# A tenth seven-product pair ahead of the attention, and low weight parts added up by a DMA

## Chip, cores and metric

The kernel runs on one core of one Trainium2 chip. The metric is the device time of one execution in microseconds. The kernel before took 1343.89 us, the median of 3 runs (1341.61 to 1345.63).

## What is computed

One layer of a decoder trunk on 1024 tokens with 1024 channels, in float32. An input projection gives queries, keys and values for two token mixers and two blocks of 1024 gate columns. One mixer is differential attention (4 heads, full causal softmax), the other a sliding-window attention (8 heads, window 128). Each mixer's output goes through its own matrix and is weighted by the sigmoid of its gates; the two are summed, mixed and added to the input. A gated MLP with a short convolution and a last norm follow.

```python
xn = rmsnorm(x, norm_mix_w[l])
proj = xn @ w_in[l]
da_q, da_k, da_v, sw_q, sw_k, sw_v, g_da, g_sw = split_cols(proj)
y_da = diff_attention(da_q, da_k, da_v, lam, lam_init, subln_w[l])
y_sw = sliding_window_attention(sw_q, sw_k, sw_v, sinks[l])
merged = jax.nn.sigmoid(g_da) * (y_da @ w_br_da[l]) + jax.nn.sigmoid(g_sw) * (y_sw @ w_br_sw[l])
x = x + merged @ w_mix_out[l]
```

## The kernel before

Data is kept transposed: channels on the 128 partitions, tokens along the row. Every float32 operand of a large product is split into a high part (a copy rounded to float32r, by ScalarE) and a low part (the operand minus its high part, by VectorE), and a product is three matmuls of 128x512: high by high, high by low, low by high (`mm3`, L202 to L211; the same in `product`, L906 to L923).

The 34 column blocks of the input projection, 128 columns each, are numbered 0 to 33; 18 to 33 are the 16 gate blocks, in the code simply "gates". `plan` (L280) sorts them into three kinds:

- `plain`: five blocks, computed directly at the start.
- `pairs`: two blocks at a time by a Strassen-like scheme of seven products (P1 to P7) of half size in place of eight. A pair takes 7 products x 4 chunks of channels x 3 matmuls = 84 matmuls; two blocks alone take 2 blocks x 2 halves of the tokens x 8 chunks x 3 = 96. The sums of weights that the scheme needs are made by GpSimd (`sum_pair`, L93, four additions a pair at L103 and L107 to L109), the high and low parts by ScalarE and VectorE (`split_pair`, L112, lines 127 and 128), and VectorE puts the seven products together (`recombine`, L454, seven additions, and one copy by ScalarE). A pair of gates is then stored to memory (`gd`) from SP's queue, L448.
- the remaining gates (23 to 33, eleven of them): computed directly, but later, between the steps of the attention. `back_half` (L559) computes one half of one gate: 24 matmuls, a copy out of PSUM by ScalarE (L565) and a store to `gd` from ScalarE's queue (L566).

`HALVES` says how many such halves are written behind each step of the attention: the first entry before it starts, then six rows of eight steps (four heads of differential attention, `u` = 0 to 3, and two groups of sliding-window heads, `u` = 4 and 5), and the last entry behind the attention, while its output is loaded. A scheduler then fixes each engine's order ahead of time, in the priority in which the code is written but taking later work that is ready where an engine would stand idle; so the halves do not stay where they are written.

A weight block is loaded by `load_w` (L167): raw weights by a DMA on SP's queue into one of three `raw` buffers, the high part by ScalarE (`wh`, L174), the low part by VectorE (`wl`, L176). Both have two buffers, and `ahead` (L70) starts the next block's loading when the present one is begun. The kernel before issues no DMA from GpSimd.

A step of differential attention (`da_step`, L622) is two score products, a masked minimum on VectorE (L640), the exponential on ScalarE (L641), a combination on VectorE (L646), transposes on TensorE (L652) and again high and low parts (L654, L655); every second step ends in the product with the values (`da_av`, L657). A sliding-window step (`sw_step`, L713) does the same for four heads; one head's scaling is done by GpSimd (L738, three others on the same line by VectorE). GpSimd also clears a part of each `aT` tile (L619). The stacks of queries and keys (`u` tiles, L576 and L586) come from memory (`qd`) and take the place of operands of the projection.

After the attention, `rest` (L766) loads the gates back (`gr`, L793), scales them on GpSimd (L794), and merges the two branches.

Of the kernel before, what the change touches and what calls it, by code (L numbers as in the profile page):

```python
# [10 lines left out]
F32 = mybir.dt.float32  # L11
F32R = mybir.dt.float32r
AF = mybir.ActivationFunctionType
ALU = mybir.AluOpType
# [6 lines left out]
KC = D // P  # L21
# [12 lines left out]
HOLD = 1  # L34
LAM_INIT = 0.2

HALVES = ((2,), (0, 0, 0, 0, 1, 1, 0, 0), (0, 0, 0, 0, 1, 0, 0, 1), (0, 0, 0, 0, 1, 0, 1, 0), (0, 0, 0, 1, 1, 0, 1, 0), (1, 0, 0, 1, 0, 1, 1, 0), (1, 0, 1, 1, 0, 0, 1, 0), (3,))
NEGMASK = 1e30


# [4 lines left out]
class Trunk:  # L45
# [121 lines left out]
    def load_w(self, src, nk=KC, eng=None, pool=None, raw=None):  # L167

        nc = self.nc
        if raw is None:  # L170
            raw = self.load_raw(src, nk)
        pool, h, l = pool or (self.wp, "wh", "wl")
        wh = self.tl(pool, [P, nk, P], h, F32R)
        self.hi = nc.scalar.copy(wh, raw)  # L174
        wl = self.tl(pool, [P, nk, P], l, F32R)
        self.lo = (eng or nc.vector).tensor_tensor(wl, raw, wh.bitcast(F32), ALU.subtract)  # L176
        return wh, wl

# [101 lines left out]
    def plan(self):  # L280

        self.kind = {m: "q" if m < 4 or 12 <= m < 16 else "k" if m < 8 or m == 16 else "v" if m < 18 else "g" for m in range(34)}


        self.plain = [0, 4, 8, 18, 20]
        self.pairs = [(1, 5), (9, 2), (6, 10), (3, 7), (11, 12), (13, 16), (17, 14), (15, 19), (21, 22)]
        gates = list(range(23, 34))
        self.back = []
        todo = [(m, hf) for m in gates for hf in range(2)]
        for steps in HALVES:  # L290
            self.back.append([[todo.pop(0) for _ in range(n)] for n in steps])
        assert not todo
        src = [(self.w_in[m], KC) for m in self.plain]
        src += [((self.w_in[a], self.w_in[b]), "pair") for a, b in self.pairs]
        src += [(self.w_in[m], KC) for m in gates]
        src += [(self.w_br[m], KC) for m in range(KC)]
        self.mix_order = [m for k in range(4) for m in (k, k + 4)]
        src += [(self.w_mix[m], KC) for m in self.mix_order]
        src += [((self.w_up[j], self.w_up[j + NF]), "pair") for j in range(NF)]


        n = N1 // 2
        self.pieces = [(m, c) for m0 in (4, 0) for c in range(2) for m in range(m0, m0 + 4)]
        src += [(self.w_dn[m:m + 2, :, n * c:n * c + n, :].rearrange("m p k c -> p m k c"), 2 * n) for m, c in self.pieces[::2]]
        pairs = [(self.w_dn[m, :, N1:N1 + 8, :], self.w_dn[m + 4, :, N1:N1 + 8, :]) for m in range(4)]
        src.insert(len(src) - 2, (pairs[0], "sums"))
        src += [(self.w_dn[m, :, N1:N1 + 8, :], 8) for m in range(4)]
        src += [(pairs[0], "rest")] + [(p, "pair", True, 1) for p in pairs[1:]]
        src += [((self.w_dn[m, :, N2:, :], self.w_dn[m + 4, :, N2:, :]), "second", m) for m in range(4)]
        src += [(self.sd[m], 8) if m < 2 else (self.sd[m], "idle") for m in range(4)]  # L310
        self.wsrc, self.wq, self.deep = src, [], False
# [1135 lines left out]
```

## Time and profile before

| | us |
|---|---|
| median of 3 runs | 1343.89 |
| lowest, highest of them | 1341.61, 1345.63 |
| the profiled execution, its own time | 1342.84 |
| its span, first to last instruction | 1340.6 |
| outside the span | 2.2 |

The page of the profile gives the busy time of each engine (PE is TensorE, PEld its weight loads, DVE VectorE, ACT ScalarE, POOL GpSimd, SP the engine that issues most DMAs), the span in 40 slices, the chain of work that ended last, and the costliest groups of instructions. Matmul records overlap, since a matmul starts before the one ahead of it has drained: the pace of TensorE is read from the starts, not from the durations. The table of windows gives each engine's busy time in a chosen stretch of the span. Projection with its pairs runs to 239 us, the attention to about 506, the merging of the branches to about 600.

### The profile page before, as it was taken

How to read it: one execution, taken by the hardware profiler on the slowest of the kernel's cores; microseconds unless marked ns; L12 is line 12 of the kernel's file. 1: busy time of each engine (PE TensorE's matmuls, PEld its weight loads, DVE VectorE, ACT ScalarE, POOL GpSimd, SP SyncE). 2: the span in 40 equal slices, each digit the busy share in tenths (PEclk: the TensorE clock that was granted, in tenths of full speed). 3: DMA queues.
4: the chain of work that ended last, by engine and by line, in shares of the span. 5: the costliest groups of instructions: out<-in, count | busy, mean ns of one | idle time of the engine just before them, and what ended most of it. 6: DMA issues, size and time to landing. Idle time of an engine off the chain costs nothing.

```text
span 1340.6 us, 17301 instructions
## 1 busy us (share of the span) xinstructions
PE 1319.9 (98%) x6264; PEld 1097.0 (82%) x6264; DVE 1069.3 (80%) x1605; ACT 621.2 (46%) x1019; POOL 497.0 (37%) x365
## 2 busy tenths in 40 slices
PE   8999999999999999999999999999999999999997
PEld 6888888888888777878888888888888888888787
DVE  8847775289889876465678999999999997978985
ACT  9432232276667765333444443444443444323454
POOL 0336553001102124651446555655565510215422
PEclk9999999999999999999999999999999999999998
DMA  7423443876553235334432222222222229671333
GB/s 258 145 107 143 156 158 141 246 182 186 144 135 124 97 119 203 141 110 157 126 110 95 78 95 79 94 68 90 90 85 80 85 82 337 214 263 63 112 124 126
DMA packets 63045, 182.64 MB, mean 136 GB/s; under 512 B 6896, under 2 KB 15216, under 8 KB 62960
## 3 DMA queue, kind: packets, MB, share of 16 engines
q1 hardware_dynamic: 51504, 164.13, 37.5%
q10 hardware_dynamic: 11456, 17.41, 3.6%
q8 instruction: 49, 0.80, 0.3%
q14 instruction: 36, 0.29, 0.1%
HBM read 130.66 MB, written 50.86 MB: 135 GB/s over the span
## 4 chain that ended last, share of the span: by engine, by line
PE 87%; POOL 4%; DVE 4%; DMA 3%; ACT 1%; issue 1%; POOLq 0%; SPq 0%; ACTq 0%; DVEq 0%
PE t L920 13%; PE t L921 13%; PE t L922 13%; PE g L209 3%; PE t L914 3%; PE g L210 3%; PE g L211 3%; PE sc L636 3%; PE y L1159 2%; PE d L1159 2%; DMA gr<-gd 2%; PE sc L211 2%; PE sc L209 2%; PE sc L210 2%; PE d L920 2%; PE d L921 2%
## 5 line engine op out<-in xcount | busy, mean ns | idle before, releaser
L1089 ACT ACTIVATE c<-us,vecs 128x512 f32<-128x512 f32 x80 | 61.3, 780 | 133.2 <-POOL us L1083 129.2
L1091 DVE SCALAR_TENSOR_TENSOR c<-us,vecs,c 128x512 f32<-128x512 f32 x160 | 110.4, 747 | 8.6 <-ACT c L1089 8.5
L1083 POOL TENSOR_TENSOR us<-us,rstd 128x1024 f32<-128x1024 f32 x38 | 99.7, 2643 | 4.5 <-DVE us L469 2.4
L128 DVE TENSOR_TENSOR sl<-sf,sh 128x1024 fp32r<-128x1024 f32 x62 | 87.6, 1415 | 11.5 <-ACT sh L127 11.5
L127 ACT CAST sh<-sf 128x1024 fp32r<-128x1024 f32 x62 | 63.3, 1048 | 60.2 <-PE t L921 43.7
L176 DVE TENSOR_TENSOR wl<-raw,wh 128x1024 fp32r<-128x1024 f32 (+2 forms) x46 | 55.7, 1210 | 31.8 <-ACT wh L174 20.2
L128 DVE TENSOR_TENSOR wl<-raw,wh 128x1024 fp32r<-128x1024 f32 (+1 forms) x35 | 76.3, 2180 | 3.7 <-ACT wh L127 3.6
L103 POOL TENSOR_TENSOR sf<-rv 128x512 f32<-128x512 f32 x30 | 41.3, 1378 | 100.9 <-DVE sl L128 57.8
L174 ACT CAST wh<-raw 128x1024 fp32r<-128x1024 f32 (+2 forms) x46 | 46.1, 1001 | 61.8 <-PE sc L210 30.5
L209 PE MATMUL g<-xh,wh 128*128 128x512 f32 x176 | 70.6, 401 | 0.1
L211 PE MATMUL g<-xh,wl 128*128 128x512 f32 x176 | 70.3, 400 | 0.0
L210 PE MATMUL g<-xl,wh 128*128 128x512 f32 x176 | 70.3, 399 | 0.0
L108 POOL TENSOR_TENSOR sf<-raw,rv 128x512 f32<-128x512 f32 x30 | 40.7, 1358 | 65.3 <-DVE sl L128 65.3
L619 POOL MEMSET aT<- 128x128 f32 x32 | 6.2, 206 | 151.6 <-PE t L665 101.3
L640 DVE CUSTOM_DVE_ANT_0 L<-sc,bias 128x128 f32<-128x128 f32 (+7 forms) x64 | 47.7, 751 | 17.0 <-PE sc L636 13.7
L641 ACT ACTIVATE L<-L,sm 128x128 f32<-128x128 f32 (+7 forms) x64 | 49.6, 778 | 20.0 <-DVE sm L640 17.3
L794 POOL TENSOR_TENSOR gr<-gr,rstd 128x1024 f32<-128x1024 f32 x16 | 40.6, 2540 | 42.5 <-DMA gr<-gd 42.3
L1093 ACT ACTIVATE c<-c 128x512 f32<-128x512 f32 x40 | 24.0, 599 | 60.7 <-DVE c L1091 60.7
L128 DVE TENSOR_TENSOR wl<-rv,wh 128x512 fp32r<-128x512 f32 x30 | 49.3, 1642 | 3.5 <-ACT wh L127 3.5
L636 PE MATMUL sc<-u,u 128*128 128x512 f32 (+2 forms) x192 | 49.8, 358 | 0.0
L211 PE MATMUL sc<-mh,wl 128*128 128x512 f32 x126 | 49.1, 390 | 0.5 <-DVE wl L176 0.5
L209 PE MATMUL sc<-mh,wh 128*128 128x512 f32 x126 | 49.0, 389 | 0.0
(527 smaller groups left out, 4400.3 us busy)
## 6 DMA issues: line engine op xcount, KB each, us to landing
u<-qd SPq DMA_DIRECT2D x72, 256.0 KB, 6.6
raw<-in_w_in SPq DMA_DIRECT2D x25, 512.0 KB, 4.2
raw<-in_w_up SPq DMA_DIRECT2D x23, 512.0 KB, 3.5
hr<-hd SPq DMA_DIRECT2D x46, 256.0 KB, 4.9
hd<-c SPq DMA_DIRECT2D x22, 512.0 KB, 2.6
rv<-in_w_up SPq DMA_DIRECT2D x21, 512.0 KB, 3.5
raw<-in_w_down SPq DMA_DIRECT2D x19, 512.0 KB, 4.2
gr<-gd SPq DMA_DIRECT2D x16, 512.0 KB, 3.7
```

Of the source, the lines that this page charges most:

```text
L127: i = nc.scalar.copy(hi, src)
L128: j = nc.vector.tensor_tensor(lo, src, hi.bitcast(F32), ALU.subtract)
L209: nc.tensor.matmul(ps, wh[:, kc + o, :], ah, start=first and n == 0, stop=False)
L210: nc.tensor.matmul(ps, wh[:, kc + o, :], al, start=False, stop=False)
L211: nc.tensor.matmul(ps, wl[:, kc + o, :], ah, start=False, stop=last and n == len(kcs) - 1)
L636: nc.tensor.matmul(sc[:, lo + n0:lo + n1], qs, k[c][part][:, n0:n1], start=part == 0, stop=part == 1)
L920: nc.tensor.matmul(ps, ah[:, k, :], bh, start=first and n == 0, stop=False, skip_group_check=skip)
L921: nc.tensor.matmul(ps, ah[:, k, :], bl, start=False, stop=False, skip_group_check=skip)
L922: i = nc.tensor.matmul(ps, al[:, k, :], bh, start=False, stop=last and n == len(ks) - 1, skip_group_check=skip)
L1083: (nc.vector if j == 0 else nc.gpsimd).tensor_tensor(u[:, 2:], u[:, 2:], self.rstd, ALU.mult)
L1089: nc.scalar.activation(c, u[:, o + 2:o + 2 + H2], AF.Identity, bias=self.vecs[:, C_CB + m:C_CB + m + 1], scale=col(m, 2))
L1091: nc.vector.scalar_tensor_tensor(c, u[:, o + k:o + k + H2], col(m, k), c, ALU.mult, ALU.add)
```

## The change

Gates 23 and 24 become a tenth pair, computed ahead of the attention. Nine gates (25 to 33) stay behind it, so 18 halves in place of 22: `HALVES` loses one in each of the rows of `u` = 0, 3, 4 and 5. For the last seven of these gates (27 to 33) the low part is made in another way: ScalarE writes the negated high part into the low part's tile, and a DMA issued by GpSimd adds the raw weights to it there. Gates 25 and 26 keep VectorE's subtraction, and so does every other weight.

```diff
-HALVES = ((2,), (0, 0, 0, 0, 1, 1, 0, 0), (0, 0, 0, 0, 1, 0, 0, 1), (0, 0, 0, 0, 1, 0, 1, 0), (0, 0, 0, 1, 1, 0, 1, 0), (1, 0, 0, 1, 0, 1, 1, 0), (1, 0, 1, 1, 0, 0, 1, 0), (3,))
+HALVES = ((2,), (0, 0, 0, 0, 0, 1, 0, 0), (0, 0, 0, 0, 1, 0, 0, 1), (0, 0, 0, 0, 1, 0, 1, 0), (0, 0, 0, 0, 1, 0, 1, 0), (1, 0, 0, 1, 0, 0, 1, 0), (1, 0, 0, 1, 0, 0, 1, 0), (3,))
...
         wl = self.tl(pool, [P, nk, P], l, F32R)
+        if eng == "adding":
+            nc.scalar.mul(wl, wh.bitcast(F32), -1.0)
+            nc.gpsimd.dma_start(wl, raw, accum_op=ALU.add)
+            return wh, wl
         self.lo = (eng or nc.vector).tensor_tensor(wl, raw, wh.bitcast(F32), ALU.subtract)
...
-        self.pairs = [(1, 5), (9, 2), (6, 10), (3, 7), (11, 12), (13, 16), (17, 14), (15, 19), (21, 22)]
-        gates = list(range(23, 34))
+        self.pairs = [(1, 5), (9, 2), (6, 10), (3, 7), (11, 12), (13, 16), (17, 14), (15, 19), (21, 22), (23, 24)]
+        gates = list(range(25, 34))
...
-        src += [(self.w_in[m], KC) for m in gates]
+        src += [(self.w_in[m], KC) for m in gates[:2]] + [(self.w_in[m], KC, "adding") for m in gates[2:]]
```

## The prediction

> **What bounds the kernel.** I read the page first: the busy times and the chain that ended last.
>
> ```profile
> span 1340.6 us, 17301 instructions
> PE 1319.9 (98%) x6264; PEld 1097.0 (82%) x6264; DVE 1069.3 (80%) x1605; ACT 621.2 (46%) x1019; POOL 497.0 (37%) x365
> PE 87%; POOL 4%; DVE 4%; DMA 3%; ACT 1%; issue 1%; POOLq 0%; SPq 0%; ACTq 0%; DVEq 0%
> ```
>
> TensorE sets the time nearly everywhere. An average hides what a stage leaves to the other engines, so next the table of windows, cut at the last three pairs, the wait for the attention's stacks (239 to 269), the four heads `u` = 0 to 3, the two sliding-window groups and the merging. Columns: stretch, its length, busy time of PE, PEld, DVE, ACT, POOL with counts, granted clock, DMA share, GB/s.
>
> ```profile
> 201.00:220.00 19.00, 19.00 (x86) 15.73 (x85) 12.30 (x13) 5.21 (x6) 9.87 (x5) 1.00 0.38 138
> 220.00:239.00 19.00, 19.00 (x85) 15.74 (x84) 10.49 (x17) 3.52 (x5) 1.28 (x6) 1.00 0.39 139
> 239.00:269.00 30.00, 30.00 (x142) 24.89 (x141) 6.32 (x16) 7.34 (x17) 0.20 (x2) 1.00 0.97 265
> 269.00:299.00 30.00, 30.00 (x189) 26.11 (x188) 28.27 (x76) 22.20 (x53) 1.24 (x7) 1.00 0.75 188
> 299.00:335.00 36.00, 36.00 (x236) 32.03 (x234) 31.16 (x82) 24.61 (x58) 3.75 (x12) 1.00 0.66 179
> 335.00:368.00 33.00, 32.95 (x211) 28.50 (x211) 28.91 (x73) 22.57 (x52) 3.02 (x8) 1.00 0.56 148
> 368.00:404.00 36.00, 35.97 (x242) 32.08 (x240) 31.04 (x91) 22.74 (x58) 3.45 (x8) 1.00 0.55 140
> 404.00:452.00 48.00, 46.92 (x271) 38.16 (x271) 40.89 (x151) 35.03 (x104) 9.21 (x10) 1.00 0.37 121
> 452.00:506.00 54.00, 53.38 (x271) 42.03 (x270) 43.07 (x136) 37.48 (x98) 12.38 (x9) 1.00 0.30 98
> ```
>
> Two things are to be seen. In the attention TensorE is full (idle 0.05 + 0.03 + 1.08 + 0.62 = 1.78 us from 269 to 506), but VectorE is close behind it: 28.27 + 31.16 + 28.91 + 31.04 + 40.89 + 43.07 = 203.3 us of those 237, or 86%. The gates are what keeps TensorE full there. And from 239 to 269 VectorE has little to do and the DMA engines are at 0.97: the stacks are loading, and gates fill TensorE.
>
> TensorE's pace is read from starts in its timeline, since records overlap:
>
> ```profile
> 219.97 0.39 PE L920 MATMUL t<-xh,wh 128*128 128x512 f32 x1
> 239.01 0.39 PE L209 MATMUL g<-xh,wh 128*128 128x512 f32 x1
> 249.89 0.38 PE L606 MATMUL t<-ident,f 128*128 128x128 f32 x2
> ```
>
> The last pair runs from 219.97 to 239.01, 19.04 us for its 84 matmuls, 0.2267 us each. The 48 matmuls of the first gate take 239.01 to 249.89, 10.88 us, the same pace. So both forms of work run undisturbed at it.
>
> **The pair.** Four halves leave the attention: 4 x 24 x 0.2267 = 21.8 us of TensorE work. A pair is added ahead of it: 19.04 us. Net 12 matmuls, **-2.72 us**, if both stretches stay full. For the pair that holds. What it needs from the other engines:
>
> ```profile
> L108 POOL TENSOR_TENSOR sf<-raw,rv 128x512 f32<-128x512 f32 x30 | 40.7, 1358 | 65.3 <-DVE sl L128 65.3
> L128 DVE TENSOR_TENSOR sl<-sf,sh 128x1024 fp32r<-128x1024 f32 x62 | 87.6, 1415 | 11.5 <-ACT sh L127 11.5
> L467 DVE TENSOR_TENSOR us<-t,u 128x512 f32<-128x512 f32 x31 | 21.4, 691 | 0.9
> ```
>
> Four additions on GpSimd (5.4 us), three and a half low parts (about 5 us) and seven additions (4.8 us) on VectorE. The parts of the tenth pair are made while the ninth is computed (220 to 239: VectorE 10.49 of 19, GpSimd 1.28), and both are pairs of gates without the extra splitting that keys and queries need. The pair before that left VectorE 12.30 of 19 with TensorE full, so I cost this at nothing; without cover the dearest piece is one subtraction of 1.4 us. Its stores to `gd` go from SP ahead of the stacks, as the ninth pair's do now.
>
> **The low parts.** What is replaced, and the load that is nearest to the new DMA:
>
> ```profile
> L176 DVE TENSOR_TENSOR wl<-raw,wh 128x1024 fp32r<-128x1024 f32 x10 | 12.1, 1215 | 13.2 <-PE t L606 11.0 <-ACT wh L174 2.2
> L174 ACT CAST wh<-raw 128x1024 fp32r<-128x1024 f32 x37 | 38.8, 1049 | 50.1 <-PE sc L210 30.5 <-PE g L210 8.1 <-PE d L921 4.7
> DMA to landing us min/median/max: 2.6/4.0/9.0
> 250.94 1.23 DVE L176 TENSOR_TENSOR wl<-raw,wh 128x1024 fp32r<-128x1024 f32 x1 [11.04 <-PE t L606]
> 261.97 0.39 PE L209 MATMUL g<-xh,wh 128*128 128x512 f32 x1
> ```
>
> The first row is of 239 to 506 alone, the third of the 512 KB weight loads of L164, the last two of the timelines. Seven subtractions, 7 x 1.215 = 8.5 us, leave VectorE between 269 and 506 (of the ten rows two lie before 269, one is of the weights behind the gates). ScalarE gets seven more passes, 7 x 1.049 = 7.3 us: its sum there is 164.6 us of 237, and 171.9 of 215 is 80%, still below VectorE. No row shows a DMA that GpSimd issues and that adds. By the loads it lands 2.6 to 9.0 us after issue; I take 9.0 for the first, which falls into the stretch with the DMA engines at 0.97. The third gate's low part was ready at 252.2, and its first matmul ran at 261.97 (the 97th of the gates): 9.8 us of slack against 1.05 + 9.0 - 1.2 = 8.9 us. Hidden, barely; later gates have a half's spacing more. Issuing costs GpSimd something unknown: nothing at the low end, at the high end a whole pass over such a tile, the 2.54 us of L794 below, seven times, on an engine that is busy 33 of 237 us.
>
> The wait that comes with it: the DMA waits on GpSimd's queue for ScalarE's second pass. Behind it stand the clearing of `aT` and one head's scaling.
>
> ```profile
> POOL aT L619 <- PE t L665: 101.3, 14, 34.7
> L738 POOL TENSOR_SCALAR L<-L,sw 128x256 f32<-128x256 f32 x14 | 14.3, 1024 | 58.2 <-DVE sw L735 30.2 <-DVE sw L729 8.9 <-PE t L755 8.7
> L794 POOL TENSOR_TENSOR gr<-gr,rstd 128x1024 f32<-128x1024 f32 x16 | 40.6, 2540 | 42.5 <-DMA gr<-gd 42.3
> SPq L164 <- DVE wl L176: 69.9, 6, 20.4
> 494.99 3.58 SPq L793 DMA_DIRECT2D gr<-gd x2
> ```
>
> GpSimd waits for others there far more than they for it, so I price that at 0, with 4 late gates x 2.5 us = 10 us, if each pass held up a sliding-window step, as its far end. The raw buffer is held until the DMA has read it, and SP's queue waits for those buffers (fourth row); behind the longest waits stand only weights and then the loads of L793, and the last wait before them is for a weight that VectorE still subtracts. Price 0.
>
> By the Trainium skill, DMA: Bandwidth & Descriptors, section Anatomy of one DMA — SWDGE (gpsimd) path, such a DMA takes about 2.0 us plus its bytes over 436 GB/s, an estimate of 3.2 us here; by it the sum would be the same. The skill speaks against the change in SBUF — State Buffer, section Who interferes with whom: a VectorE instruction in a two-port mode locks GpSimd out, and a DMA from GpSimd then waits for its descriptors. That rule is the rival "late low parts" below; no row of this trace shows such a wait, since GpSimd issues none.
>
> **The attention with fewer gates.** This is the disputed term. From 269 on VectorE keeps 203.3 - 8.5 = 194.8 us of work, and TensorE wants to be through in 237 - 21.8 = 215.2. That asks VectorE for a share of 90.5%, now 85.8%. What share it can reach bounds the price from both sides. At 94.2%, the row 269 to 299 with TensorE full, it needs 206.8 us: price 0. At 88.4%, the mean of the four heads (119.4 of 135), 220.4: price 5.2. In those heads TensorE, not VectorE, was the limit, so 88.4% is a floor rather than a ceiling; but they include the slack places between heads that will not go away. I take the middle, **+2.5 us**.
>
> **Sum.** 1342.84 - 2.72 + 2.5 = **1342.6 us** against the profiled execution's own time, itself 1.05 below the median of the runs, 1343.89. A measurement of this kernel can tell about 0.3%, 4 us, from no change; the forecast is no change that can be told.
>
> **Rivals.**
> 1. *The softmax takes over: slower.* VectorE's share stays at 85.8%, because its idle time is a step's own chain (minimum, exponential, transposes, two parts) and not TensorE's queue. Then 194.8 / 0.858 = 227.0 us, price 11.9: 1342.84 - 2.72 + 11.9 = **1352.0**. For it: in the two sliding-window stretches VectorE is at 84 of 102 us, and TensorE already idles 1.70. Against it: TensorE runs its queue in order, with gates ahead of the attention's own matmuls, so part of that idle time is the gates' doing. It is slower by over 0.3% from a share of 87.8% down (221.9 us, price 6.7).
> 2. *The relief wins: faster.* VectorE's lighter load ends the 1.78 us of idle TensorE too, and nothing opens: 1342.84 - 2.72 - 1.78 = **1338.3**. For it: the sliding-window stretches hold four of the seven subtractions. Against it: it asks for 90.5% without a gap.
> 3. *Late low parts: slower.* GpSimd is held up, by VectorE or by its own queue, and the DMA lands after twice the longest load, 18.0 us. The third gate's low part is then 1.05 + 18.0 - 1.2 - 9.8 = 8.1 us late, while there are only gates to run: 1342.6 + 8.1 = **1350.7**. Against it: 9.8 us of slack, and the scheduler can put score products first.
> 4. *The pair doesn't gain what it says.* Its parts come late and the 2.72 us are lost in its first products: **1345.3**. Against it: TensorE full in the stretch at 12.30 of 19 us of VectorE and 9.87 of GpSimd.
>
> **Chances.** Forecast 0.43 (1340 to 1346), rival 1 0.26, rival 2 0.18, rival 3 0.06, rival 4 0.07. Faster by over 0.3% (below 1339.9) needs rival 2 nearly whole: 0.17. Slower by over 0.3% (above 1347.9): most of rivals 1 and 3, 0.28. Within: 0.55. The range goes from rival 2 to rival 1: 1338.3 to 1352.0.
>
> **What would show it.** After: a tenth stretch of 19.0 us ahead of the first gate, which starts at 258; VectorE at about 90% from then + 30 us to the end of the attention; the attention's end at 506 - 2.7 + 2.5. If VectorE's share there stays near 86% and TensorE idles over 7 us, rival 1; if TensorE waits at L211 for `wl`, rival 3; if TensorE idles under 1 us, rival 2. If the projection's end comes later than 258.2, rival 4. The step I trust least is the share of 90%.

## The result, and the profile after

| | us |
|---|---|
| after, median of 6 runs | 1354.82 (1351.43 to 1356.68) |
| before, median of 6 runs beside them | 1343.77 (1340.64 to 1345.63) |
| ratio, 95% interval | 1.0084, 1.0071 to 1.0097 |
| profiled execution after, its span | 1351.43, 1349.6 |

The change costs 0.84%, 11.05 us of the medians. The time lies above the range of the prediction, and on the side to which it gave 0.28. The profiled execution is the fastest of its six, so the traces explain 9.0 us of span (1349.6 against 1340.6), and the rest is spread between executions.

The page of the kernel after: span, busy times, and the chain that ended last.

```profile
span 1349.6 us, 17324 instructions
PE 1320.8 (98%) x6252; PEld 1096.1 (81%) x6252; DVE 1067.5 (79%) x1607; ACT 627.3 (46%) x1025; POOL 508.7 (38%) x376
PE 85%; DVE 4%; POOL 4%; DMA 3%; ACT 2%; issue 1%; POOLq 0%; SPq 0%; ACTq 0%; DVEq 0%
```

Twelve matmuls fewer, as the change says, and yet TensorE is no less busy and the span is longer: the averages of the page do not show where the time goes. TensorE's timeline after the change gives the marks: start of the last pair, first gate, first product of the merging.

```profile
238.36 0.39 PE L924 MATMUL t<-xh,wh 128*128 128x512 f32 x1
...
257.40 0.39 PE L213 MATMUL g<-xh,wh 128*128 128x512 f32 x1
...
516.02 0.39 PE L200 MATMUL sc<-yh,wh 128*128 128x512 f32 x1
```

And the last of them before the change:

```profile
506.40 0.39 PE L196 MATMUL sc<-yh,wh 128*128 128x512 f32 x1
```

The tenth pair takes 257.40 - 238.36 = 19.04 us, to the hundredth what was forecast. From the first gate to the merging the kernel took 506.40 - 239.01 = 267.39 us, and now 516.02 - 257.40 = 258.62. That is 8.77 less, where 21.8 us of gates were taken out. The first gate starts 18.39 us later, and 18.39 - 8.77 = 9.6 us are lost by the merging; behind it 0.6 come back. All of the loss lies between the attention's start and its end.

The table of windows shows it. "The stretch" is from now on the time from 30 us after the first gate to the merging. Before:

```profile
269.00:506.40 237.40, 235.62 (x1409) 199.25 (x1409) 203.74 (x607) 164.73 (x420) 33.05 (x53) 1.00 0.50 140
```

After, whole, and in parts (the last one cut at 520):

```profile
287.40:516.00 228.60, 218.93 (x1319) 184.08 (x1319) 196.83 (x606) 166.69 (x423) 36.66 (x58) 0.99 0.57 153
...
387.00:423.00 36.00, 33.03 (x228) 28.52 (x228) 30.54 (x88) 23.30 (x59) 3.17 (x7) 1.00 0.50 121
423.00:470.00 47.00, 43.06 (x244) 34.26 (x243) 44.19 (x177) 37.10 (x111) 11.01 (x12) 1.00 0.42 126
470.00:520.00 50.00, 47.29 (x235) 37.30 (x234) 36.91 (x110) 36.50 (x87) 11.42 (x9) 0.97 0.43 132
```

VectorE's share was 203.74 / 237.40 = 85.8% and is 196.83 / 228.60 = 86.1%: it did not move. TensorE's idle time went from 1.8 to 9.7 us, nearly all of it in the last three parts (2.97 + 3.94 + 2.71), that is from the fourth head on. The first three heads still fill TensorE with nearly as many gate matmuls as before (129 against 136, counted in the stretches of the three heads); the fourth head holds 17 in place of 42, and the two sliding-window groups 169 in place of 231. The four halves that were taken away are missing at the end. What TensorE waits for most in the stretch, after the change:

```profile
PE t L759 <- DVE aT L753: 3.1, 5, 1.0
PE g L213 <- ACT g L569: 1.8, 2, 0.9
PE t L668 <- DVE aT L659: 1.2, 2, 0.9
```

The first and the third row are waits for the low parts of the transposed softmax weights, VectorE's work; with a smaller row of the same kind they make 4.7 us of the 9.4 that all rows of this view add up to. No row of it is a wait at L215 for `wl`. The low parts by DMA, in the groups and in the rows of `wl`:

```profile
L178 POOL DMA_DIRECT2D wl<-raw x7: 859/928/1068, 272.0 to 479.4; - x7
DMA to landing us min/median/max: 4.5/7.0/11.0
```

Issuing one costs GpSimd 0.93 us (the median of seven), and the transfer lands 4.5 to 11.0 us later. The first two are issued ahead of the stretch.

### The profile page after: what moved, and what is told of

It is laid out like the page before. It is cut to its first block, busy times and chain, and to the rows that moved or that the text cites. A ratio compares the mean times of both kernels' runs of the same rounds, so it can differ in the third digit from the quotient of the medians.

```text
span 1349.6 us, 17324 instructions
## 1 busy us (share of the span) xinstructions
PE 1320.8 (98%) x6252; PEld 1096.1 (81%) x6252; DVE 1067.5 (79%) x1607; ACT 627.3 (46%) x1025; POOL 508.7 (38%) x376
## 4 chain that ended last, share of the span: by engine, by line
PE 85%; DVE 4%; POOL 4%; DMA 3%; ACT 2%; issue 1%; POOLq 0%; SPq 0%; ACTq 0%; DVEq 0%
PE t L924 13%; PE t L925 13%; PE t L926 13%; PE t L918 3%; PE sc L640 3%; PE y L1163 2%; PE d L1163 2%; PE sc L215 2%; PE sc L213 2%; PE sc L214 2%; PE d L924 2%; PE d L925 2%; PE d L926 2%; PE g L213 2%; PE g L214 2%; PE g L215 2%
## 5 line engine op out<-in xcount | busy, mean ns | idle before, releaser
L128 DVE TENSOR_TENSOR sl<-sf,sh 128x1024 fp32r<-128x1024 f32 x64 | 89.7, 1404 | 11.9 <-ACT sh L127 11.9
L213 PE MATMUL g<-xh,wh 128*128 128x512 f32 x144 | 58.0, 403 | 1.8 <-ACT g L569 1.8
L180 DVE TENSOR_TENSOR wl<-raw,wh 128x1024 fp32r<-128x1024 f32 (+2 forms) x37 | 46.0, 1242 | 16.8 <-ACT wh L174 16.3
L215 PE MATMUL g<-xh,wl 128*128 128x512 f32 x144 | 58.2, 404 | 0.0
L214 PE MATMUL g<-xl,wh 128*128 128x512 f32 x144 | 58.0, 403 | 0.0
L215 PE MATMUL sc<-mh,wl 128*128 128x512 f32 x126 | 49.1, 390 | 0.4 <-DVE wl L180 0.4
L233 POOL TENSOR_TENSOR rs<-ms,mhalf 128x8 f32<-128x8 f32 (+2 forms) x9 | 13.7, 1527 | 94.3 <-DVE ms L231 91.4
```

The source lines that it names most:

```text
L128: j = nc.vector.tensor_tensor(lo, src, hi.bitcast(F32), ALU.subtract)
L213: nc.tensor.matmul(ps, wh[:, kc + o, :], ah, start=first and n == 0, stop=False)
L214: nc.tensor.matmul(ps, wh[:, kc + o, :], al, start=False, stop=False)
L215: nc.tensor.matmul(ps, wl[:, kc + o, :], ah, start=False, stop=last and n == len(kcs) - 1)
```

## The experiments

Two theories stood against each other. **Ceiling**: without enough gates the softmax sets the pace, and VectorE isn't busier than about 86% over the stretch, whatever the gates do (rival 1). **Transfer**: the new low parts do the harm. Within the first, it was open whether the limit is the sum of VectorE's work or the chain of steps around it.

### The two halves of the change

The pair alone (all low parts on VectorE), and the adding alone, on the kernel before:

```diff
-        src += ... [(self.w_in[m], KC, "adding") for m in gates[2:]]
+        src += [(self.w_in[m], KC) for m in gates]
```

> The tenth pair and 18 halves alone; all low parts by VectorE again. Theory A (the attention has too few gates left, and the softmax on VectorE sets its pace): VectorE gets 8.5 us back, so at least as slow as the change, 1354 to 1363 us. Theory B (the adding DMA and ScalarE's extra pass cost the time, the pair is good): 1340 to 1345 us.

```diff
+        if eng == "adding": ...
-        src += [(self.w_in[m], KC) for m in gates]
+        src += [(self.w_in[m], KC) for m in gates[:4]] + [(self.w_in[m], KC, "adding") for m in gates[4:]]
```

> Eleven gates behind the attention as before; the low parts of gates 27 to 33 by ScalarE's negation and GpSimd's adding DMA. Theory A: TensorE stays full, VectorE is relieved by 8.5 us that it didn't need, 1341 to 1345 us. Theory B: 1351 to 1356 us, nearly the whole loss.

The pair alone: 1351.79, ratio 1.0075 (1.0061 to 1.0089), which can't be told from the whole change (1.0084, 1.0071 to 1.0097). The adding alone: 1344.45, ratio 1.0013 (1.0002 to 1.0023). Both met theory A's side: the loss is the pair's, though the pair alone came out 2 us faster than the 1354 that theory A allowed. The stretch with the pair alone, and with the adding alone:

```profile
287.40:514.30 226.90, 216.31 (x1314) 181.60 (x1314) 198.47 (x605) 161.29 (x414) 32.11 (x53) 1.00 0.50 138
```

```profile
269.00:506.10 237.10, 235.42 (x1409) 198.97 (x1409) 197.22 (x599) 170.97 (x427) 39.02 (x60) 1.00 0.57 155
```

The adding does take VectorE from 203.74 to 197.22 us, but TensorE is full there, and nothing gets shorter. With the pair it could have helped, and didn't: a share of 87.5% without it, 86.1% with it. VectorE's busy time in the stretch is only 1.6 us lower with it (198.47 to 196.83): two of the seven subtractions lie ahead of the stretch in any case.

### How long the attention is with hardly a gate

Gates 27 to 33 are not computed at all (the results of 25 and 26 are stored in their places). In the second kernel the transposes also get a third PSUM buffer, taken from the gates.

```diff
+        if m > 26:
+            return
```

> The changed kernel without the products and weights of gates 27 to 33 (14 of 18 halves, 76 us of TensorE; the results of gates 25 and 26 are stored in their places). It shows how long the softmax takes with next to no gates. Theory A: from the end of the wait for the stacks to the last product with values the attention stays above 195 us, since VectorE's 195 us of work remain, so the kernel loses less than 25 us: 1330 to 1345. If the chain were not the limit (theory B), it would fall by nearly the 76 us to VectorE's work at 95%: attention 205, still, but with TensorE idle and VectorE above 93%; the share of VectorE is what tells: A 85 to 90%, B 93 to 97%.

```diff
-            self.psG = ... bufs=2 ...; self.psT = ... bufs=2 ...
+            self.psG = ... bufs=1 ...; self.psT = ... bufs=3 ...
```

> The kernel with two gates only (gates 27 to 33 left out, the results of 25 and 26 stored in their places), with three psT buffers. It shows whether the floor of 252 us that the attention kept with two gates moves. Theory A1: within 4 us of it. Theory A2 by psT: 235 to 245 us.

One run each: 1352.31 and 1353.18. Windows of the first: whole, the four heads together, and the last three of them:

```profile
287.70:513.80 226.10, 174.79 (x1005) 138.59 (x1003) 189.65 (x603) 146.40 (x394) 29.52 (x52) 0.91 0.43 114
287.70:422.00 134.30, 108.90 (x676) 89.85 (x675) 114.11 (x311) 84.83 (x205) 10.80 (x33) 0.95 0.57 143
...
318.00:354.00 36.00, 28.93 (x184) 24.47 (x184) 29.32 (x79) 22.25 (x53) 3.41 (x10) 0.95 0.56 152
354.00:388.00 34.00, 27.14 (x171) 22.33 (x170) 28.18 (x74) 21.34 (x52) 3.31 (x10) 0.95 0.47 120
388.00:422.00 34.00, 27.64 (x188) 23.28 (x188) 29.10 (x82) 21.19 (x51) 2.92 (x8) 1.00 0.46 111
```

TensorE idles 51.3 us of 226.1, and the stretch is as long as with nine gates. VectorE is at 83.9%, in the four heads at 85.0% (114.11 of 134.30 us), below the 88.4% that it showed there beside a full TensorE. The time is 7 us above what theory A allowed, and the share just under its 85 to 90%. One thing confounds it: TensorE's mean granted clock is 0.91 here, so the matmuls of the steps were slower than in the kernels with more gates, and what that adds to the 226.1 us was not measured. The last row is free of it: at a clock of 1.00 TensorE idles 6.4 of 34 us, and VectorE is at 85.6%. So at least there its idle time is not TensorE's queue. The third buffer moved the stretch by 0.5 us (225.6), as theory A1 expected. The chain of work of the kernel with two gates, in its last sliding-window steps (start, duration, what), shows what the idle time there is made of:

```profile
503.57 0.64 PE t L752 x4
...
504.29 0.59 ACT aT L755
...
504.91 0.70 DVE aT L756
...
505.65 0.52 PE t L762
...
506.25 0.59 ACT g L764
...
506.86 0.42 DVE ys L769
...
507.29 0.43 DVE ys L769
...
507.85 0.64 PE t L752 x4
```

From one transpose to the next 4.28 us pass, of which VectorE works 0.70 + 0.42 + 0.43 = 1.55. Each engine waits for the one ahead of it. These are the last steps alone; for the rest of the stretch no chain is shown here.

### More work on VectorE, ScalarE or GpSimd

From the pair alone: the seven low parts made twice on VectorE; one more pass of ScalarE ahead of each of them; and, from the whole change, GpSimd's own subtraction in place of negation and DMA.

```diff
+            nc.vector.tensor_tensor(wl, raw, wh.bitcast(F32), ALU.subtract)
```

> The pair alone, with VectorE making each of the seven low parts of gates 27 to 33 twice over: 8.5 us more of VectorE's work, beside the chain of the softmax. Theory A1 (VectorE's throughput bounds the attention: its work over a share of 88%): 9 to 10 us above the pair alone, 1360 to 1363. Theory A2 (the chain of a step bounds it, from one engine to the next, and VectorE has room): within 3 us of the pair alone, 1349 to 1355.

```diff
+            nc.scalar.mul(wl, wh.bitcast(F32), -1.0)
```

> The pair alone, with ScalarE's negation into the low part's tile put ahead of VectorE's subtraction for gates 27 to 33: ScalarE gets 7.3 us more, VectorE keeps its own, no DMA adds. Theory A1: no change against the pair alone, 1350 to 1354. Theory A2: a pass of 1.05 us now and then stands ahead of an exponential: 0 to 5 us above the pair alone. As the change itself, 1354 to 1356, would say that ScalarE's pass is what the adding costs.

```diff
-            nc.scalar.mul(wl, wh.bitcast(F32), -1.0)
-            nc.gpsimd.dma_start(wl, raw, accum_op=ALU.add)
-            return wh, wl
+            eng = nc.gpsimd
```

> The change with the seven low parts subtracted by GpSimd itself: no second pass on ScalarE, no adding DMA, VectorE relieved all the same. Theory A: as the change, 1352 to 1357. Theory B: ScalarE's 7.3 us and the landing of 4.5 to 11 us are gone, 1341 to 1347.

Measured: 1361.59, ratio 1.0135 (1.0120 to 1.0151); 1359.91, 1.0118 (1.0095 to 1.0142); 1356.04, 1.0102 (1.0088 to 1.0117). The stretches, in this order:

```profile
287.70:523.60 235.90, 219.90 (x1314) 184.05 (x1314) 203.97 (x609) 160.19 (x412) 32.00 (x53) 0.99 0.48 133
```

```profile
287.70:520.40 232.70, 219.58 (x1314) 185.70 (x1314) 200.52 (x607) 165.85 (x420) 32.11 (x53) 0.98 0.49 136
```

```profile
288.20:518.30 230.10, 216.85 (x1313) 182.81 (x1313) 199.92 (x601) 160.44 (x414) 43.82 (x58) 0.99 0.48 135
```

VectorE's share is 86.5%, 86.2% and 86.9%. Of the seven added instructions five lie in the stretch and two ahead of it, in the first two kernels. Five subtractions, 6.1 us of VectorE, go with a stretch 9.0 longer than the pair alone has it, as theory A1 expected of the time; five passes, 5.3 us of ScalarE, an engine at 71%, go with one 5.8 longer. The second was expected by neither theory: 1359.91 is 8 us above the pair alone. So passes on an engine far from full still cost about their own time here. The third kernel gives ScalarE nothing and takes the subtractions off VectorE, and it is no faster either (1356.04, as theory A expected); why is seen at the end, in what GpSimd's passes did to VectorE. That ScalarE's passes are what keeps the whole change from gaining is therefore likely, but not shown.

### The softmax unloaded

The low parts of the transposed softmax weights are left out and the high part is used twice: with the pair alone, before the change, and with two gates.

```diff
-            nc.vector.tensor_tensor(lo[:, :nj, qo:qo + P], ps[:, :nj, :], ...)
...
-            nc.vector.tensor_tensor(lo, ps, hi.bitcast(F32), ALU.subtract)
-            parts.append((hi, lo))
+            parts.append((hi, hi))
```

> The pair alone, and VectorE doesn't make the low parts of the transposed softmax weights (L655 and L749 of the kernel before); their high parts are multiplied in the low parts' place, so TensorE's work stays. It takes some 45 us of VectorE's 200 away. Theory F (the softmax engines, VectorE first, set how long the attention takes): TensorE is the bound again, its idle time there falls under 3 us, and the pair is worth its 12 matmuls: 1 to 4 us below the next kernel. Theory R (the scheduler's order spends the gates too early, whatever VectorE's load): 3 to 9 us above the next kernel.

> The kernel before with the same low parts left out: the yardstick for the run ahead of it. Both theories: TensorE is full already, so little moves, 1336 to 1343 us.

> Two gates only (27 to 33 left out, the results of 25 and 26 stored in their places) and no low parts of the transposed softmax weights (their high parts in their place). From 30 us behind the first gate to the merging the kernel with two gates took 226.1 us, with VectorE busy for 189.7. Theory T (VectorE's throughput is the floor): it falls with VectorE's work, some 155 us of it left, to TensorE's own work, 175 to 190 us. Theory C (the chain of a step is the floor, and two subtractions are a small part of it): 200 to 220 us.

Pair: 1346.28, ratio 1.0022 (1.0012 to 1.0032). Before: 1350.24, 1.0046 (1.0028 to 1.0064). Two gates: 1332.02, one run. The stretches, in this order:

```profile
287.40:505.90 218.50, 215.69 (x1315) 180.43 (x1314) 163.28 (x528) 159.96 (x416) 33.74 (x51) 1.00 0.51 144
```

```profile
269.00:509.20 240.20, 237.50 (x1407) 197.26 (x1406) 167.73 (x529) 163.72 (x420) 33.59 (x51) 1.00 0.50 139
```

```profile
287.80:494.75 206.95, 175.43 (x1002) 137.04 (x1002) 153.01 (x522) 144.70 (x394) 29.42 (x50) 0.90 0.47 123
```

With VectorE at 74.7%, taking four halves out makes the stretch 21.7 us shorter (240.2 to 218.5): the whole 21.8 of the prediction, and the pair is then 4.0 us faster than its own counterpart. That is theory F: where the softmax leaves room, the pair gains what was worked out. Two gates alone need 206.95 us, as theory C expected, with no engine above 85% but at a mean clock of 0.90: below VectorE's ceiling lies a second floor. What stays open is why the kernel before got 6.8 us slower with less work on VectorE, where 1336 to 1343 were expected; the counterpart is itself a little long. In the profiled executions 2.8 us of that lie in the stretch, and 5.4 between the start of the merging and the end of the span, where the two kernels do the same (839.6 against 834.2 us); the pair without low parts has as much there (840.0). Against the kernel before itself its stretch is 18.9 shorter.

### Work added to VectorE that nothing needs

48 reductions of 0.8 us over an idle operand are added to VectorE, one behind each step of the attention. In the first two kernels the scheduler was free to move them:

```diff
+                    nc.vector.tensor_reduce(self.side, self.bias[:, 0:640], axis=mybir.AxisListType.X, op=ALU.max)
```

> Two gates only, and one more instruction of VectorE in each of the 48 steps, a maximum over 640 columns of a constant tile, that nobody waits for: some 34 us of work beside the chain. Theory T: the stretch grows by nearly all of it, from 226.1 to 250 to 262 us. Theory C: VectorE had 36 us idle there, so it grows by under 12 us, to 238 at most.

> The pair alone without the low parts of the softmax weights, with the same side instruction in each step: VectorE gets back about what was taken away, but beside the chain. Theory T: the loss comes back, the stretch goes from 218.5 us to 225 to 232, the time to 1351 to 1358. Theory C: the stretch stays under 221, the time 1344 to 1349.

1361.09 (one run), and 1356.06, ratio 1.0093 (1.0074 to 1.0111). The two point opposite ways. With two gates the stretch is 234.55 us (VectorE 206.35 of it, 88.0%), as theory C expected; with the pair it is 226.5 (VectorE 180.71, 79.8%, TensorE idle for 6.9), as theory T expected. But the work did not lie where it was written: 21 of the 48 reductions ran ahead of the stretch, and all were done by 394 and by 354 us. With the pair TensorE idles most behind them, 3.26 of the 36 us from 387 to 423. So it counts where the work lies, and not only how much it is. The next two hold each reduction to its step.

```diff
+                    with tc.issue_after(self.step.ins):
+                        nc.vector.tensor_reduce(self.side, ...)
```

> The kernel with only gates 25 and 26 behind the attention (gates 27 to 33 are not computed, their stored results are those of 25 and 26), and 48 reductions of an idle operand added on VectorE, one or two behind each step of the attention, each held to its step: 48 x 811 ns = 38.9 us of VectorE work that nothing needs. Without that work the stretch from 30 us after the first gate to the merging is 226.1 us, with VectorE busy 189.7. Theory throughput (the attention is as long as VectorE's work divided by a share it can't exceed): the added work lengthens the stretch by 24 to 36 us, to 250 to 262. Theory chain (the attention is as long as the chain of dependent instructions of its steps, and VectorE's idle time lies in it): most of the added work falls into idle time, 238 or less, VectorE's share over 92%. By either the time is that of the kernel without the added work plus the lengthening.

> The pair alone, with the low parts of the transposed softmax weights left out (the high part is used twice), and the same 48 reductions on VectorE, held to their steps. Without them: stretch 218.5 us, VectorE 163.3 busy, 1346.3. With them VectorE has about as much to do as with the low parts (202 against 198.5 us), but the chain of a step is the shorter one. Throughput: the stretch is that of the pair alone again, 225 to 232, time 1351 to 1358. Chain: it stays at 221 or less, 1344 to 1349.

1380.10 (one run), and 1348.20, ratio 1.0044 (1.0027 to 1.0061). The stretches, in this order:

```profile
287.20:541.30 254.10, 186.16 (x1003) 148.44 (x1002) 219.10 (x648) 147.74 (x394) 29.95 (x52) 0.86 0.38 101
```

```profile
288.25:506.60 218.35, 214.21 (x1313) 181.82 (x1313) 189.44 (x575) 161.57 (x414) 33.86 (x51) 1.00 0.51 144
```

The first met what the sum of VectorE's work expects, 250 to 262: 29.5 us more busy time (219.10 against 189.65) came with a stretch 28.0 longer, at a share of 86.2%. The second met what the chain expects, 221 or less: 26.2 us more (189.44 against 163.28) cost nothing. All 48 reductions, 38.6 us by their durations, lie in the stretch in both (one of the second in part); busy time rises by less because it counts overlapping records once. The two need not contradict each other: the second began at 74.7% and came to 86.8%, so evenly spread work was free up to about the ceiling, and the first began near it (83.9%). There it cost 0.95 us for each us of busy time, or 0.73 for each us of added instructions. This price is of one run, with the mean clock down to 0.86 from 0.91, and a reduction held to its step stands in VectorE's order ahead of that step's low parts or scalings; so it may be the price of a longer chain as well as of more work.

### Three versions that might have kept the gain

From the pair alone: a third PSUM buffer for the transposes, one less for the gates; GpSimd scales two of four heads; and the halves of the gates are held behind the last transpose of their step, with another `HALVES`, so that they lie where TensorE would wait.

```diff
-            self.psG = ... bufs=2 ...; self.psT = ... bufs=2 ...
+            self.psG = ... bufs=1 ...; self.psT = ... bufs=3 ...
```

> The pair alone with three PSUM buffers for transposes and products with the values (psT) and one for the gates (psG; the merging behind it uses psT). Theory A1: as the pair alone, 1349 to 1355. Theory A2, with the two psT buffers as the narrow place of the chain: 5 to 12 us below the pair alone, 1339 to 1347.

```diff
-            eng = nc.gpsimd if h in (3,) else nc.vector
+            eng = nc.gpsimd if h in (2, 3) else nc.vector
```

> The pair alone, with two heads of four scaled by GpSimd in a sliding-window step in place of one: 16 x 0.456 = 7.3 us leave VectorE where TensorE idles, and GpSimd gets 16 us. Theory F by VectorE's work alone: 4 to 8 us below the pair alone, 1344 to 1348. If what GpSimd takes over comes back as a longer step (its pass is 1.02 us against 0.46), no gain or a loss: 1351 to 1357.

```diff
+        with self.tc.issue_after(self.step.ins) if self.step is not None else nullcontext():
             self.mm3(ps, self.pw, self.xact, hf)
```

> The pair alone with the gates held: each half is issued on TensorE only behind the last transpose of its step, and the 18 halves are written 5 ahead of the attention, one in each of the first three heads, two in the fourth, three in each sliding-window group, two behind it. Theory F: the attention is as long as the softmax makes it, 1349 to 1356. Theory R: the idle time of the fourth head and the sliding-window steps goes, 1341 to 1347.

1372.69 (1.0217, 1.0202 to 1.0233), 1354.15 (1.0080, 1.0064 to 1.0096) and 1395.09 (1.0391, 1.0370 to 1.0411). The first and the last are slower than either of their theories allowed. With one buffer the stretch is 245.1 us; the gates wait for ScalarE's copy, but for 4.1 us only, of 20.2 that TensorE idles, so that does not explain it. GpSimd's second head takes VectorE to 195.90 us (2.6 less, where 7.3 were worked out) of a stretch of 227.0, no shorter than 226.9. Held gates are worst, at 272.5 us. Another placing of the 18 halves without holding them was not tried, so it is not shown that the loss comes from the number of gates alone and not also from where they lie. No kernel here that computes the whole layer is faster than the kernel before.

## Why the prediction was wrong, step by step

- **The pair, -2.72**: right. The pair takes 19.04 us after the change, and with the softmax unloaded four halves are worth 21.7 of the 21.8 us (against a counterpart that is itself 2.8 us longer than the kernel before).
- **The pair's preparation, price 0**: right. No more is lost ahead of the first gate than the pair's own time: 18.39 us.
- **The low parts**: nearly right. They land after up to 11.0 us instead of 9.0, and TensorE never waits for them; VectorE got 6.5 us of relief with the adding alone, and 1.6 in the stretch beside the pair, where five of the seven subtractions lie, in place of the 8.5 worked out; adding alone costs 0.13% (0.02 to 0.23), 1.7 us. That ScalarE's 7.3 us cost nothing was wrong where gates are short: the same passes, beside VectorE's subtractions, came with a stretch 5.8 us longer than the pair alone has.
- **GpSimd and SP, price 0**: TensorE waits for neither in the stretch after the change; rival 3 did not happen.
- **The attention with fewer gates, +2.5**: this step failed. It measures 21.8 - 8.77 = 13.0 us. The step took the middle between a share of 94.2%, read from 30 us at the start, and 88.4%, read from heads with TensorE full, and called the second "a floor rather than a ceiling" because TensorE was the limit there. With two gates TensorE idles 19% of the four heads, and VectorE's share in them is 85.0%: 88.4% was no floor. Over the stretch the share is 84 to 88% in ten kernels whose gates don't fill TensorE (the two with two gates, the pair, the change, and six with work added or moved), and lower in three: 82.0% with one gate buffer, 79.8% with the early reductions, 75.7% with held gates. None reaches the 90.5% that the prediction asked for. What the gates left over was not VectorE's to take.
- **Rival 1** named it: share 85.8%, stretch 227.0, price 11.9, 1352.0. Measured: 86.1%, 228.6, 13.0, and a time of 1354.82 (1351.43 in the profiled execution). Its sign from the sliding-window groups, where TensorE already idled 1.70 us at 84 of 102 us of VectorE, was the one to trust, and its bound was met: TensorE idles 9.7 us, over the 7 that the prediction set. The argument against it ("part of that idle time is the gates' doing") fell with the two-gate kernel, in the head where the clock stayed at 1.00. That its 1352.0 lies so near the 1351.43 is in part luck: its price was 1.1 us too low, and 0.65 us ahead of the first gate and 0.6 behind the merging, which it did not count, made up for that.
- Not settled is what the ceiling is made of. The chain in the last steps, the price of ScalarE's passes and the 206.95 us that remain without the low parts speak for the steps' dependences; that VectorE work added near the ceiling costs 0.73 to 0.95 for 1 speaks for VectorE's own order. Both could hold if VectorE's instructions lie on the chain nearly all the time; no run here tests that directly.

## What to carry to other kernels

Filler work on a full engine hides how long the other engines' chain is: before taking filler away, look for the length of that stretch without any of it, by an experiment that leaves it out. A share that an engine shows beside a full TensorE is no floor: it may already be above what the engine holds once the filler is gone, and the stretches where TensorE already idles a little tell that first. And where the steps of a chain set the pace, moving work from the busiest engine to another need not gain anything: here the stretch was 226.9 us without such a move, and 227.0 to 230.1 with the three that were tried.

## What the runs showed of the hardware

TensorE's granted clock falls where it idles a little at a time. With two gates its mean goes down along the sliding-window groups, though the longest of its waits up to 510 us was 2.6 us (windows, and the largest row of its waits: total, times, longest):

```profile
422.00:470.00 48.00, 37.31 (x214) 29.01 (x212) 42.47 (x172) 33.60 (x109) 9.79 (x11) 0.93 0.27 89
470.00:490.00 20.00, 15.10 (x72) 11.86 (x73) 17.48 (x71) 12.91 (x41) 3.69 (x4) 0.83 0.09 26
490.00:510.00 20.00, 12.77 (x49) 7.67 (x47) 14.72 (x47) 13.36 (x39) 3.29 (x4) 0.74 0.17 53
```

```profile
PE t L752 <- DVE L L745: 7.6, 4, 2.6
```

So lost filler can cost twice, since the chain's own matmuls run at that clock; what this adds was not measured. The Trainium skill, TensorE: Matmul & The Clock Gate, section Part 1: The HAM clock gate (the "warmup" mystery), says that the gate halves the clock after at least one idle window of about 3.4 us; the fall agrees in direction, but waits of 2.6 us and less were enough here.

GpSimd's own subtraction, in the groups of the kernel that tried it:

```profile
L178 POOL TENSOR_TENSOR wl<-raw,wh 128x1024 fp32r<-128x1024 f32 x7 | 16.7, 2389 | 35.7 <-ACT wh L174 34.6 <-ACT y L669 1.2
```

One takes 2.39 us against VectorE's 1.22, and VectorE's busy time did not fall for it (199.92 us in its stretch against 198.47 with the subtractions on VectorE). The timeline shows why:

```profile
478.23 2.35 POOL L178 TENSOR_TENSOR wl<-raw,wh 128x1024 fp32r<-128x1024 f32 x1 [1.17 <-ACT wh L174]
478.26 2.34 DVE L736 TENSOR_TENSOR sw<-sw 128x4 f32<-128x4 f32 x1
```

A VectorE instruction over 128x4 elements, 0.16 us in the median of its 16, took 2.34 us and ended with GpSimd's pass. At 442.90 the same line took 1.52 us and again ended with the pass, at 445.3, and two of L648 (three operands, all in SBUF) were 0.7 and 1.9 us longer than usual, while L751 and L729, which read PSUM, kept their usual 0.69 and 0.41 us beside a pass. These four instructions alone give back 6.1 us, as much as the five subtractions that had left the stretch.
